# Matmuls of zeros at the head of a kernel: rounds of whole and half-array matmuls on two banks instead of twelve whole ones

## The chip, the cores and the metric

The kernel runs on one core of one Trainium2 chip. The metric is the device time of one execution in microseconds (us); the time of a kernel is the median of several executions.

A core has five engines that run side by side and wait for each other by semaphores: TensorE (PE in the profile, with its weight loads as PEld), VectorE (DVE), ScalarE (ACT), GpSimd (POOL) and SyncE (SP), which here issues the transfers.

## What is computed

One layer of a hybrid streaming encoder, for a prompt of 1024 positions and a sample of 32, with shared weights (D = 1024):

```python
hn = rmsnorm(h, g_pre)
qa, ka, va, ga, qb, kb, vb, gb = split(hn @ w_in)      # w_in: 1024 x 4096
oa = band_attention(qa, ka, va, rel_bias)              # 8 heads x 64, chunks of 64, 8 chunks back
ob = stick_breaking(qb, kb, vb)                        # 8 heads x 64, strictly causal
y  = concat(oa * silu(ga), ob * silu(gb)) @ w_out
h  = h + rmsnorm(y, g_post)
h  = h + sigmoid(h @ w_ple_gate) * (p @ w_ple)
```

The outputs are the two h and the new keys and values. All is float32. The change touches none of these values: it stands in matmuls whose results nobody reads.

## The kernel before

The function stream_step (from line 809 on it holds the whole kernel) does not issue instructions itself. Each call such as `nc.tensor.matmul` is recorded by a Recorder, which notes what each operation reads and writes; `emit` then plays them in an order that a planner finds (`order`, `simulate`): a list schedule with modelled durations, due times, and a table of offsets by engine and tile name (AHEAD_OF, AHEAD_AT). Every instruction is issued from one line, so the profile shows nearly all of them as L809, and one tells them apart by the names of their tiles.

PSUM, which matmuls write, is used as eight banks of 128 x 512. A tile of a bank is asked for with `psum(tag, name)`; the planner hands banks out as they come free, with a reserve for each tag.

The places that the prediction speaks of, in the order of PE's program:

- `zeros` (L1387, L1388): a tile of 128 x 256 that DVE sets to zero. `idle` is a bank; twelve matmuls (L1390, L1391) multiply zeros by zeros into it. They wait for DVE alone, and they are PE's first instructions.
- `ptp` (L1588 to L1591): eight transposes of the first prompt tiles of p, loaded into `pp`, against `ident`. ACT and DVE split their result into a high and a low part, `php`. The p and x tiles, weights and gains arrive by transfers that SP issues from the start on.
- `gpre` (L1818 to L1823): four matmuls that spread the gain g_pre over all partitions; they are told to follow the transposes.
- `ple` (from L1614 on): products of php with w_ple, whose two halves (`wph`, `wpl`) are made by ACT, POOL and DVE (wph0True and wpl0True among them).
- `ptx`: transposes of the normed x tiles. For each tile ACT sums squares (`be`), POOL makes the reciprocal root (`rs`), DVE scales by it and by gpre (`be<-be,rs,gpre`), and PE transposes.
- `mm_kA`, `mm_qA`, `mm_vA` and so on: the input projection, three products per weight (high by high, low by high, high by low), then between them the scores (`SA`, `SB`), the weights' transposes (`ptw`) and values (`PVA`, `PVB`) of the attention, and those of the sample (`SsA`, `PVsA`, `PVsB`). `PVsA<-newsA` and `PVsB<-newsB` multiply the 32 new positions, and so use 32 rows of the array.

The matmuls of zeros are not in the reference; they occupy PE until the first input has come.

```python
    zeros = at.tile([P, 2 * P], F32R, tag="ot", name="zeros", bufs=3)
    nc.vector.memset(f(zeros), 0.0)
    idle = psum("PV", "idle")
    for _ in range(12):
        nc.tensor.matmul(idle[:, 0:256], zeros[:, 0:P], zeros, start=True, stop=True)
```

Of the kernel before, what the change touches and what calls it, by code (L numbers as in the profile page):

```python
# [13 lines left out]
P = 128  # L14
# [3 lines left out]
T = SEQ + NS  # L18
# [4 lines left out]
HD = 64  # L23
# [791 lines left out]
def stream_step(  # L815
# [7 lines left out]
    nc = rec  # L823
# [7 lines left out]
    def psum(tag, name):  # L831
        return ps.tile([P, 512], F32, tag=tag, name=name, bufs=8)
# [554 lines left out]
    zeros = at.tile([P, 2 * P], F32R, tag="ot", name="zeros", bufs=3)  # L1387
    nc.vector.memset(f(zeros), 0.0)  # L1388
    idle = psum("PV", "idle")
    for _ in range(12):  # L1390
        nc.tensor.matmul(idle[:, 0:256], zeros[:, 0:P], zeros, start=True, stop=True)  # L1391

    def sample_attention(ab, gi):

# [774 lines left out]
    for m, (nm, src, group) in enumerate(sets):  # L2169
# [3 lines left out]
        for n, prod in enumerate(ORDER):  # L2173
            for pair, t in enumerate(group):
# [24 lines left out]
                bank = psum("S", f"{nm}{t}{prod}")  # L2199
# [126 lines left out]
```

## Time and profile before

| | |
|---|---|
| time, median of 3 runs | 753.23 us (753.18, 753.23, 753.71) |
| the profiled execution's own time | 752.74 us |
| its span, first to last instruction | 751.0 us |
| mean granted clock of TensorE | 0.998 |
| PE busy | 743.3 us, 4314 matmuls |
| DVE, ACT, POOL busy | 601.9, 532.7, 435.8 us |
| first matmul of zeros, first transpose behind them | 2.24, 4.97 us |

The profile is of one execution. A row of its timeline gives the start in us from the first instruction, the length, the engine, the tiles (written <- read), the shape, how many instructions of a kind the row merges, and, in brackets, how long the engine stood idle before it and for what. A matmul's shape such as `32*128 32x256` gives the rows and columns of the array that it uses, and then its moving operand. Matmuls overlap, so that a row's length holds the tail of its last one, and the distance between two matmuls' starts is what PE's pace is read from. A row of the stretches gives PE's, PEld's, DVE's, ACT's and POOL's busy time, the granted clock, the share of the transfer engines and GB/s.

### The profile page before, as it was taken

The page shows a single profiled execution, that of the slowest core. Times are in us where ns is not written, and L with a number is a line of the kernel's source. Part 1 is how long each engine was busy: PE and PEld are TensorE (multiplying, and loading weights), DVE is VectorE, ACT ScalarE, POOL GpSimd, SP SyncE. Part 2 cuts the span into 40 slices and gives each one's busy share as a digit, 9 for nine tenths or more (in the row PEclk, how much of TensorE's full clock was granted, in tenths as well). Part 3 has the DMA queues.
Part 4 walks back from the last instruction along what each step waited for, and adds up shares of the span by engine and source line. Part 5 has one row for each costly group of instructions (what it writes and reads, how often), then busy time and mean ns, then how long its engine had stood idle before and what let it go on. Part 6 is the DMA issues. An engine that isn't in the chain of part 4 may idle for free.

```text
span 751.0 us, 13763 instructions
## 1 busy us (share of the span) xinstructions
PE 743.3 (99%) x4314; PEld 683.5 (91%) x4314; DVE 601.9 (80%) x989; ACT 532.7 (71%) x1099; POOL 435.8 (58%) x551
## 2 busy tenths in 40 slices
PE   8999999999999999999999999999999999999997
PEld 7999999999999989999999999999997877888786
DVE  6827777889889989887989897888365878998965
ACT  5748785978877879886878866644348877784642
POOL 5723546773374742567763448687634268698623
PEclk9999999999999999999999999999999999999999
DMA  8745998868998768899788898999879847669654
GB/s 308 230 124 138 262 254 271 232 186 240 219 291 225 212 214 236 238 281 270 207 243 245 204 235 236 290 276 262 273 237 332 285 136 270 216 193 369 224 173 140
DMA packets 198971, 177.90 MB, mean 237 GB/s; under 512 B 66145, under 2 KB 158281, under 8 KB 198898
## 3 DMA queue, kind: packets, MB, share of 16 engines
q1 hardware_dynamic: 198898, 177.02, 80.8%
q8 instruction: 34, 0.56, 0.3%
q14 instruction: 39, 0.32, 0.1%
HBM read 112.01 MB, written 65.20 MB: 236 GB/s over the span
## 4 chain that ended last, share of the span: by engine, by line
PE 98%; DVE 1%; ACT 0%; issue 0%; DVEq 0%
PE mm_vA L809 6%; PE mm_kA L809 6%; PE mm_qA L809 6%; PE mm_vB L809 6%; PE mm_gB L809 6%; PE mm_kB L809 6%; PE mm_gA L809 6%; PE mm_qB L809 6%; PE SB L809 5%; PE PVB L809 4%; PE PVA L809 4%; PE SA L809 4%; PE ple L809 3%; PE o1P L809 3%; PE g1P L809 3%; PE o3P L809 3%
## 5 line engine op out<-in xcount | busy, mean ns | idle before, releaser
L809 POOL TENSOR_TENSOR be<-be 128x512 f32<-128x512 f32 (+5 forms) x98 | 92.8, 959 | 39.8 <-DVE be L809 21.6
L809 DVE TENSOR_TENSOR_SCAN be<-be,unit 128x383 f32<-128x383 f32 (+8 forms) x100 | 92.4, 945 | 12.8 <-ACT be L809 12.2
L809 ACT ACTIVATE be<-SB 128x384 f32<-128x384 f32 (+4 forms) x192 | 82.5, 501 | 15.5 <-PE SB L809 6.5
L809 DVE TENSOR_TENSOR wTl<-be,wTh 128x640 fp32r<-128x640 f32 (+4 forms) x72 | 68.4, 970 | 8.7 <-ACT wTh L809 8.4
L809 DVE STREAM_TRANSPOSE be<-be 128x640 f32<-128x640 f32 (+4 forms) x80 | 64.5, 815 | 6.0 <-POOL be L809 4.3
L809 ACT CAST wTh<-be 128x640 fp32r<-128x640 f32 (+4 forms) x72 | 50.7, 732 | 9.6 <-DMA be<-swapB 6.7
L809 ACT ACTIVATE be<-be,statA 128x640 f32<-128x640 f32 (+2 forms) x64 | 44.4, 695 | 6.2 <-DVE statA L809 6.0
L809 DVE CUSTOM_DVE_ANT_0 be<-SA,biasA 128x320 f32<-128x320 f32 (+2 forms) x64 | 29.7, 478 | 5.1 <-PE SA L809 4.6
L809 PE MATMUL SB<-kl,LB 128*128 128x384 f32 (+5 forms) x96 | 32.8, 343 | 0.0
L809 PE MATMUL SB<-kdB,LB 128*128 128x384 f32 (+5 forms) x96 | 32.7, 343 | 0.0
L809 PE MATMUL SA<-kdA,LA 128*128 128x320 f32 (+2 forms) x96 | 30.4, 318 | 0.0
L809 PE MATMUL SA<-kl,LA 128*128 128x320 f32 (+2 forms) x96 | 30.3, 319 | 0.0
L809 POOL TENSOR_TENSOR oB<-oB,oB 128x256 f32<-128x256 f32 x32 | 27.4, 875 | 4.4 <-DMA oB<-in_w_out_dram 4.3
L809 POOL TENSOR_TENSOR gB<-gB,gB 128x256 f32<-128x256 f32 x32 | 25.2, 808 | 5.9 <-DMA gB<-in_w_ple_gate_dram 5.8
L809 PE MATMUL PVB<-wTh,v2B 128*128 128x512 f32 (+2 forms) x96 | 25.9, 342 | 0.0
L809 POOL TENSOR_TENSOR kl<-stkA,kdA 64x512 fp32r<-64x512 f32 (+2 forms) x16 | 18.5, 1163 | 9.5 <-ACT kdA L809 7.2
L809 POOL TENSOR_TENSOR h<-h,x 128x512 f32<-128x512 f32 (+1 forms) x18 | 23.0, 1299 | 1.4 <-DVE h L809 1.2
L809 PE MATMUL PVB<-wTl,v2B 128*64 128x128 f32 (+2 forms) x96 | 23.0, 348 | 0.0
L809 PE MATMUL mm_kB<-hnl,wh_kB 128*128 128x352 f32 x96 | 22.4, 333 | 0.0
L809 POOL TENSOR_TENSOR kl<-stkB,kdB 64x512 fp32r<-64x512 f32 x16 | 18.3, 1159 | 7.1 <-ACT kdB L809 4.0
L809 PE MATMUL mm_qA<-hnl,wh_qA 128*128 128x352 f32 x96 | 22.1, 332 | 0.0
L809 PE MATMUL PVA<-wTl,v2A 128*64 128x128 f32 (+1 forms) x96 | 22.1, 312 | 0.0
(678 smaller groups left out, 2562.6 us busy)
## 6 DMA issues: line engine op xcount, KB each, us to landing
swapB<-be SPq DMA_DIRECT2D x16, 448.0 KB, 4.5
be<-swapB SPq DMA_DIRECT2D x64, 112.0 KB, 3.4
swapA<-be SPq DMA_DIRECT2D x8, 640.0 KB, 3.6
swapA<-be SPq DMA_DIRECT2D x16, 320.0 KB, 5.1
be<-swapA SPq DMA_DIRECT2D x32, 160.0 KB, 5.4
be<-swapA SPq DMA_DIRECT2D x64, 80.0 KB, 3.8
oB<-in_w_out_dram SPq DMA_DIRECT2D x16, 256.0 KB, 5.2
sum_dro<-oB SPq DMA_DIRECT2D x16, 256.0 KB, 3.2
```

The costliest lines, as they stand in the source:

```text
L809: getattr(getattr(tc.nc, o.what[0]), o.what[1])(*args, **kw)
```

## The change

The twelve matmuls become three rounds of four on two banks: a whole one into `idle`, a whole one into `other`, then one on rows 0 to 63 into `idle` and one on rows 64 to 127 into `other`. HD is 64. Columns, weights' width and the moving 256 columns stay as they are.

```diff
     idle = psum("PV", "idle")
-    for _ in range(12):
-        nc.tensor.matmul(idle[:, 0:256], zeros[:, 0:P], zeros, start=True, stop=True)
+    other = psum("T", "other")
+    for _ in range(3):
+        for bank, r in ((idle, slice(0, P)), (other, slice(0, P)), (idle, slice(0, HD)), (other, slice(HD, P))):
+            nc.tensor.matmul(bank[:, 0:256], zeros[r, 0:P], zeros[r], start=True, stop=True)
```

On all engines the other instructions keep their order and, but for one, their waits. The first place is PE's start. Before, with the waits in brackets (DMAHW: a transfer; ptp_254 and ptp_265 are the two banks of transposes):

```order
L809 MATMUL idle<-zeros 128x256 [waits DVE_49]
L809 MATMUL idle<-zeros 128x256 x11
L809 MATMUL ptp_254<-ident,pp_180 128x128 [waits DMAHW0_49,Pool_49]
L809 MATMUL ptp_254<-ident,pp_180 128x128 x3
L809 MATMUL ptp_265<-ident,pp_180 128x128 [waits DMAHW2_49]
```

Now, from the last of the three rounds on; these rows give the written side's shape, so the third and fourth, which are the halves, read like the whole ones:

```order
L809 MATMUL idle<-zeros 128x256
L809 MATMUL other<-zeros 128x256
L809 MATMUL idle<-zeros 128x256
L809 MATMUL other<-zeros 128x256
L809 MATMUL ptp_264<-ident,pp_180 128x128 [waits DMAHW0_49,Pool_49]
L809 MATMUL ptp_264<-ident,pp_180 128x128 x3
L809 MATMUL ptp_266<-ident,pp_180 128x128 [waits DMAHW2_49]
```

Nothing behind the zeros has moved; the number of matmuls is the same.

The second place is PE's first products of ple, a few instructions on (ple_0_307 and ple_0_308 before are ple_0_308 and ple_0_309 now). Before:

```order
L809 MATMUL ple_0_307<-wph0True,php_190 128x512 [waits Activation_49]
L809 MATMUL ple_0_307<-wph0True,php_190 128x512 [waits DVE_49]
L809 MATMUL ple_0_308<-wph0True,php_190 128x512 x2
L809 MATMUL ple_0_315<-wph0True,php_192 128x512 [waits Activation_49]
L809 MATMUL ple_0_315<-wph0True,php_192 128x512 [waits DVE_49]
```

Now:

```order
L809 MATMUL ple_0_308<-wph0True,php_190 128x512 [waits Activation_49]
L809 MATMUL ple_0_308<-wph0True,php_190 128x512 [waits DVE_49]
L809 MATMUL ple_0_309<-wph0True,php_190 128x512 [waits PE_49]
L809 MATMUL ple_0_309<-wph0True,php_190 128x512
L809 MATMUL ple_0_316<-wph0True,php_192 128x512 [waits Activation_49]
```

The banks are handed out differently, now that two are taken at the start, and ple_0_309 gets the one of `idle`; it waits for the last matmul of zeros into it.

## The prediction

> **What bounds the kernel now.** I read the first page first: the share of each engine and the chain that ended last.
>
> ```profile
> span 751.0 us, 13763 instructions
> PE 743.3 (99%) x4314; PEld 683.5 (91%) x4314; DVE 601.9 (80%) x989; ACT 532.7 (71%) x1099; POOL 435.8 (58%) x551
> PE 98%; DVE 1%; ACT 0%; issue 0%; DVEq 0%
> ```
>
> TensorE (PE) is busy for 743.3 of 751.0 us and carries 98% of the chain, so whatever makes PE late by some time at the start makes the end late by that time, unless PE later waits for something that did not move. The waits of PE behind the first 20 us, and the two places they stand at, are:
>
> ```profile
> PE SsA L809 <- DVE QhlsA L809: 0.5, 1, 0.5
> PE mm_vA L809 <- ACT stvA L809: 0.2, 1, 0.2
> ...
> 411.71 0.39 PE L809 MATMUL SsA<-Kh0sA,QhlsA 128*128 128x272 f32 x1 [0.46 <-DVE QhlsA L809]
> ...
> 266.73 0.59 PE L809 MATMUL mm_vA<-hnh,wh_vA 128*128 128x352 f32 x2 [0.19 <-ACT stvA L809]
> ```
>
> Together 0.65 us (0.46 + 0.19): the most that could be absorbed later. Next I read the timeline of PE in the first 30 us, since the change stands at its first row.
>
> ```profile
> 2.24 2.93 PE L809 MATMUL idle<-zeros 128*128 128x256 f32 x12 [2.24 <-DVE zeros L809]
> 4.97 1.91 PE L809 MATMUL ptp<-ident,pp 128*128 128x128 f32 x8
> 6.53 1.64 PE L809 MATMUL gpre<-wTl,ones 128*128 128x512 f32 x4
> 8.00 1.55 PE L809 MATMUL ple<-wph0True,php 128*128 128x512 f32 x6
> 9.39 0.86 PE L809 MATMUL ple<-wpl0True,php 128*128 128x512 f32 x3
> ...
> 14.50 0.60 PE L809 MATMUL ptx<-ident,be 128*128 128x128 f32 x4
> ...
> 19.48 1.08 PE L809 MATMUL ptx<-ident,be 128*128 128x128 f32 x8
> 20.32 0.71 PE L809 MATMUL ple<-wph0True,php 128*128 128x512 f32 x2
> ```
>
> PE runs without a hole from 2.24 us. Its rate changes, though. Eight transposes took 4.97 to 6.53, 0.195 us each; eight of the same form took 19.48 to 20.32, 0.105 each. Twelve matmuls of zeros, 256 columns, took 2.73 us; six matmuls of 512 columns took 8.00 to 9.39, 0.232 each, which is 0.116 for 256. So PE works at half its rate at first. The four gpre matmuls took 1.47 us, between 4 x 0.427 (half rate) and 4 x 0.232: c/0.427 + (1.47 - c)/0.232 = 4 gives c = 1.19 us at half rate, so the rate doubles at about 7.7 us, some 5.5 us after the first matmul. The granted clock of the page does not show this (it reads 1.00 there); it shows the way back at the end:
>
> ```profile
> 743.00:746.00 3.00, 3.00 (x26) 2.91 (x24) 1.71 (x3) 0.81 (x2) 1.55 (x2) 1.00 0.24 89
> 746.00:748.23 2.23, 0.17 (x2) 0.00 (x0) 1.86 (x5) 0.57 (x2) 0.79 (x1) 1.00 0.26 96
> 748.24:748.26 0.02, 0.00 (x0) 0.00 (x0) 0.02 (x1) 0.00 (x0) 0.00 (x0) 0.50 1.84 717
> ```
>
> PE stops at 746.17 (0.17 us into the second stretch), and at 748.24 the clock falls to 0.50: the half rate is a clock gate that follows PE's activity.
>
> **The change part by part.** The instructions of all engines keep their order; only the twelve matmuls change, and one wait is added (the first ple_0_309 waits for the last zeros on its bank). That producer is done some 2 us earlier, so I cost the wait at nothing. So the change is a matter of two numbers: when the zeros end, and when the gate opens.
>
> (a) *Whole against half, switching.* Six times now PE goes from all 128 rows to fewer or back (three rounds, in and out, the last way out to ptp). The trace has no matmul on 64 rows, but some on 32, between whole ones:
>
> ```profile
> 213.64 0.28 PE L809 MATMUL PVsA<-Vl2sA,whsA 128*128 128x256 f32 x1
> 213.76 0.28 PE L809 MATMUL PVsA<-Vh2sA,wlsA 128*128 128x256 f32 x1
> ...
> 271.35 0.28 PE L809 MATMUL PVsB<-Vh2sB,wlsB 128*128 128x256 f32 x1
> 271.56 0.38 PE L809 MATMUL PVsB<-newsB 32*128 32x256 f32 x1
> 271.86 0.43 PE L809 MATMUL mm_vA<-hnh,wl_vA 128*128 128x352 f32 x1
> 272.22 0.50 PE L809 MATMUL PVsB<-newsB 32*128 32x256 f32 x2
> 272.65 0.60 PE L809 MATMUL mm_vA<-hnl,wh_vA 128*128 128x352 f32 x2
> ...
> 271.55 0.18 PEld L809 LDWEIGHTS PVsB<-newsB 32*128 32x128 f32 x1 [0.17 <-issue]
> ```
>
> Whole to whole, 256 columns take 0.12 us (213.64 to 213.76). Across a change of rows, start to start is 0.21 (271.35 to 271.56): 0.09 more. The weights are then loaded only at 271.55, not ahead of time, and the matmul behind them lasts 0.38 instead of 0.28: 0.10 more. So a switch costs about 0.19 us at the full clock. At half clock the exposed load is shown by the first zeros matmul, which had nothing ahead of it:
>
> ```profile
> L809 PEld LDWEIGHTS idle<-zeros x12: 288/330/333, 2.2 to 4.5; 128*128 128x128 f32 x12
> L809 PE MATMUL idle<-zeros x12: 415/415/582, 2.2 to 4.8; 128*128 128x256 f32 x12
> ```
>
> 582 against 415 ns is 0.167 us; the others are (2.73 - 0.167) / 12 = 0.213 apart. The stop itself lies between 0.09 (full clock) and 0.415 - 0.213 = 0.20 (the whole tail of a matmul); I take 0.11, near the first, the only one measured at a switch. So 6 x (0.11 + 0.167) = 1.66 us; bounds 6 x 0.19 = 1.14 and 6 x 0.367 = 2.20.
>
> (b) *Two halves side by side.* The second half's rows are others than the first's, so it may run beside it: a pair saves between nothing and 0.213 us. If its load follows the first half's by 0.167, it starts 0.167 instead of 0.213 later and saves 0.046; I take that, 3 x 0.046 = 0.14, bounds 0 and 0.64. [...]
>
> (c) *Sum.* The zeros end 1.66 - 0.14 = 1.5 us later, ptp starts at 6.47 (bounds: 1.14 - 0.64 = 0.5 and 2.2 later). Up to the gate's opening at 7.7 all of that is work at half rate, and PE does it afterwards in half the time: PE is 0.75 us late (0.25 to 1.1), if the gate opens when it did. The other way, a shorter row of zeros would be of use, since its successor is not waiting for data:
>
> ```profile
> 0.72 0.40 SPq L809 DMA_DIRECT2D pp<-in_p_prompt_dram  x1
> ...
> 1.53 0.35 SPq L809 DMA_DIRECT2D pp<-in_p_prompt_dram  x1
> DMA to landing us min/median/max: 2.6/2.9/3.2
> ```
>
> The two loads of pp have landed by 0.72 + 3.2 = 3.9 and 1.53 + 3.2 = 4.7 at the latest, before 4.97.
>
> What hangs behind ptp is late by more than PE: ACT's first cast of php, with it the casts and subtractions on POOL, by 1.5 us.
>
> ```profile
> 7.25 1.29 POOL L809 TENSOR_TENSOR wpl0True<-wpr_0True,wph0True 128x512 fp32r<-128x512 f32 x1 [5.44 <-ACT wph0True L809]
> 11.58 0.72 POOL L809 TENSOR_SCALAR rs<-ms 128x1 f32<-128x1 f32 x1
> 12.99 1.41 DVE L809 SCALAR_TENSOR_TENSOR be<-be,rs,gpre 128x512 f32<-128x512 f32 x2
> 14.11 0.22 POOL L809 TENSOR_SCALAR rs<-ms 128x1 f32<-128x1 f32 x1 [1.16 <-ACT be L809]
> ```
>
> POOL works through from 7.25 to rs at 11.58, so the first half of DVE's scaling (12.99 to 13.7) would end at about 15.2; PE wants it for ptx at 14.50 + 0.75 = 15.25. The cover just holds; for each 0.1 us that the zeros are later still, 0.05 is added there. POOL's idle 1.16 us before 14.11 takes up the rest.
>
> PE's own time: 752.74 us (span 751.0 and 1.7 around it) + 0.75 = 753.5. The median of the runs shown is 753.23, 0.49 above that execution, so I put **754.0** against it.
>
> **The rivals.**
>
> *The gate opens later (slower).* With six stops, PE streams about 2.4 us of the 4.2 us of zeros. Place: the clock from 2.24 to 12 us. It decides if the gate wants unbroken work: steady work opened it after 5.5 us, and an idle 2.07 us (746.17 to 748.24) closed it. If those 5.5 count from the last switch at 6.47, it opens at 12.0 instead of 7.7; PE does 4.3 us at half rate, 2.1 us of work lost, with 0.75 about 2.9: 756.1. For it: the work before the opening was entirely unbroken. Against: ptp and gpre, most of what came before the opening, are unchanged. [...]
>
> *Halves run side by side and switching is free.* The zeros are 0.64 us shorter, PE 0.3 ahead: 752.9. The rows at 271 us speak against it.
>
> *The lateness is absorbed* at 266.73 and 411.71: at most 0.65, 753.3. Against it: what PE waits for there comes from PE's own earlier work.
>
> *The gate opens earlier*, as the halves might count as more activity: PE is then held by x; ptx cannot start before DVE's 13.7, 0.8 earlier than 14.50: 752.4. Nothing in the trace speaks for it.
>
> **How the numbers follow.** Forecast 0.48 (753.23 + 0.25 to + 1.1: 753.5 to 754.3); gate later 0.34; free switching 0.11; absorbed 0.05; gate earlier 0.02. What a measurement of this kernel can tell from no change is about 0.2%, 1.5 us. Slower by more: the late gate and a little of the forecast's upper end, 0.38. Faster by more: 0.02, what is left for an earlier gate whose gain x does not hold back. Within: 0.60, the rest. The range leaves out the two cases below 753.1 (0.13) and reaches to the late gate: 753.1 to 756.1.
>
> **What would show it.** Right: idle matmuls on 64 rows in the timeline, the stretch from the first zeros to ptp 4.2 us instead of 2.73, ple's first row near 8.75, and every later stage late by the same 0.75. If ple's six take 2.6 us (0.43 each) instead of 1.39, the gate is late. If ptp starts before 4.97, switching is free and the forecast wrong in sign. If a later stage differs by another amount than ple's first row, the lateness was absorbed or grew.

## The result, and the profile after

| | before | after |
|---|---|---|
| median of 6 runs each, us | 753.20 (752.38 to 754.25) | 755.52 (754.69 to 757.21) |
| ratio after / before | | 1.0032, 95% interval 1.0019 to 1.0045 |
| profiled execution, its span | 752.74, 751.0 | 755.65, 753.9 |

The change makes the kernel slower by 2.4 us (0.0032 x 753.2; 1.4 to 3.4 by the interval). The time lies inside the range that was given, 1.5 us above the forecast. First the page of after: span, busy time, and the head of the chain of work that ended last.

```profile
span 753.9 us, 13763 instructions
PE 745.4 (99%) x4314; PEld 683.8 (91%) x4314; DVE 600.8 (80%) x989; ACT 532.4 (71%) x1099; POOL 435.9 (58%) x551
PE 94%; DVE 2%; DMA 2%; ACT 1%; issue 1%; DVEq 0%; ACTq 0%; SPq 0%
```

The other engines' busy time is as before within about 1 us. PE is busy for 2.1 us more (745.4 against 743.3), and the chain leaves PE for some more of its way (94% instead of 98%): two things to look for. PE's timeline at the start of after, and a later row of before to compare with:

```profile
2.24 0.58 PE L809 MATMUL idle<-zeros 128*128 128x256 f32 x1 [2.24 <-DVE zeros L809]
2.62 0.41 PE L809 MATMUL other<-zeros 128*128 128x256 f32 x1
2.97 0.58 PE L809 MATMUL idle<-zeros 64*128 64x256 f32 x1
2.97 0.58 PE L809 MATMUL other<-zeros 64*128 64x256 f32 x1
3.48 0.58 PE L809 MATMUL idle<-zeros 128*128 128x256 f32 x1
...
4.71 0.58 PE L809 MATMUL idle<-zeros 128*128 128x256 f32 x1
...
5.94 1.97 PE L809 MATMUL ptp<-ident,pp 128*128 128x128 f32 x8
7.56 2.05 PE L809 MATMUL gpre<-wTl,ones 128*128 128x512 f32 x4
9.41 2.16 PE L809 MATMUL ple<-wph0True,php 128*128 128x512 f32 x6
11.42 0.86 PE L809 MATMUL ple<-wpl0True,php 128*128 128x512 f32 x3
...
23.11 1.46 PE L809 MATMUL mm_kA<-hnh,wh_kA 128*128 128x352 f32 x8
```

```profile
21.10 1.46 PE L809 MATMUL mm_kA<-hnh,wh_kA 128*128 128x352 f32 x8
```

A round takes 1.23 us (3.48 to 4.71), where four whole matmuls took 4 x 0.213 = 0.85. The two halves of a pair start together (both at 2.97). ptp starts at 5.94 instead of 4.97. Before, the six matmuls of ple ran at full rate from the first on (8.00 to 9.39, 1.39 us); now they take 9.41 to 11.42, 2.01 us, and gpre's four take 1.85 (7.56 to 9.41) instead of 1.47. So PE works at half rate (0.43 us from one matmul of 512 columns to the next, 8.99 to 9.41, against 0.232 at full rate before) for longer: it is 0.97 us late at ptp, 1.41 at ple's first row, 2.03 at ple's next rows (11.42 against 9.39), and still 2.01 at mm_kA (23.11 against 21.10). From there to 409 us it stays at 2.0 to 2.1.

The gate's closing can be seen in the stretches of time at the end (us, then busy time of PE, PEld, DVE, ACT, POOL, granted clock, DMA share, GB/s):

```profile
748.50:751.42 2.92, 0.57 (x5) 0.36 (x4) 2.10 (x6) 0.78 (x2) 1.18 (x1) 1.00 0.31 112
751.42:751.44 0.02, 0.00 (x0) 0.00 (x0) 0.00 (x0) 0.00 (x0) 0.00 (x0) 0.60 1.06 358
```

It closes at 751.42, before at 748.24. The trace also has a record of the moments at which the granted clock changes, from which the opening can be read: 7.55 us before, 10.73 after. PE's pace bears the record out: the opening of after falls among ple's six, which take 2.01 us, neither the 1.39 of full rate nor the 2.6 of half rate. Opening and closing moved by the same 3.18 us; the experiments say why.

The second place where the traces part lies in the middle. PE's waits in after, the row of the longer one, and the same row of before:

```profile
PE SA L809 <- DVE wlsA L809: 1.2, 1, 1.2
PE mm_vA L809 <- ACT stvA L809: 0.2, 1, 0.2
...
427.40 0.39 PE L809 MATMUL SA<-kdA,LA 128*128 128x320 f32 x1 [1.16 <-DVE wlsA L809]
```

```profile
424.70 0.31 PE L809 MATMUL SA<-kdA,LA 128*128 128x320 f32 x1
```

The wait of 0.46 for QhlsA at 411.71 is gone, so that there PE is only 1.37 late; in its place it waits 1.16 for wlsA before 427.40 (424.70 before, 2.70 earlier), and is 2.9 late from 434 us to the end. So of the 2.9 us of this pair of executions, 2.03 arise in the first 12 us, 0.80 between 409 and 434 us, and the rest between 266 and 280 us.

### The profile page after: what moved, and what is told of

Its sections match the earlier page's. It is cut to its first block, busy times and chain, and to the rows that moved or that the text cites. A ratio compares the mean times of both kernels' runs of the same rounds, so it can differ in the third digit from the quotient of the medians.

```text
span 753.9 us, 13763 instructions
## 1 busy us (share of the span) xinstructions
PE 745.4 (99%) x4314; PEld 683.8 (91%) x4314; DVE 600.8 (80%) x989; ACT 532.4 (71%) x1099; POOL 435.9 (58%) x551
## 4 chain that ended last, share of the span: by engine, by line
PE 94%; DVE 2%; DMA 2%; ACT 1%; issue 1%; DVEq 0%; ACTq 0%; SPq 0%
PE mm_vA L809 6%; PE mm_kA L809 6%; PE mm_qA L809 6%; PE mm_vB L809 6%; PE mm_gB L809 6%; PE mm_gA L809 6%; PE mm_kB L809 5%; PE mm_qB L809 5%; PE SB L809 5%; PE PVB L809 4%; PE PVA L809 4%; PE ple L809 3%; PE SA L809 3%; PE o1P L809 3%; PE g1P L809 3%; PE o3P L809 3%
## 5 line engine op out<-in xcount | busy, mean ns | idle before, releaser
L809 ACT CAST wTh<-be 128x640 fp32r<-128x640 f32 (+4 forms) x72 | 50.7, 733 | 11.1 <-DMA be<-swapB 6.9
```

The source lines that it names most:

```text
L809: getattr(getattr(tc.nc, o.what[0]), o.what[1])(*args, **kw)
```

## The experiments

Ten runs were made, two of them with the kernels after and before unchanged. The theory in question, an assumption of the author's that the runs are to test: **the gate looks at PE's activity in windows of fixed length that run on their own; it opens at the end of the first window with enough of it, and rounds with stops don't have enough.** Its rivals: the gate opens after a fixed time or amount of work, wherever that begins; matmuls of zeros, or on half the rows, don't count as activity; the second bank or the longer zeros cost the time by themselves. (A step below is such a window.)

The record of the clock in each run's own trace gives for every kernel when it went up and came down. The last two columns are worked out: the share of a step of 3.413 us in which PE streamed columns, that is without stops and without loads that nothing covers, for the step at whose end the clock went up and for the step ahead of that one.

| kernel | up, us | down, us | down - up, in steps of 3.413 us | share, step that ended with the opening | share, step ahead |
|---|---|---|---|---|---|
| before | 7.55 | 748.24 | 217.0 | 0.99 | 0.50 |
| before, once more (e8) | 8.25 | 748.94 | 217.0 | 0.99 | 0.71 |
| after | 10.73 | 751.42 | 217.0 | 0.99 | 0.69 |
| after, once more (e7) | 9.53 | 750.22 | 217.0 | 0.99 | 0.51 |
| e1, two banks | 6.68 | 750.78 | 218.0 | 1.00 | 0.25 |
| e2, grouped | 6.81 | 750.91 | 218.0 | 0.76 | 0.29 |
| e3, seventeen | 6.81 | 750.91 | 218.0 | 1.00 | 0.29 |
| e4, zeros first | 5.29 | 749.40 | 218.0 | 0.96 | 0.16 |
| e5, rounds early | 7.26 | 751.36 | 218.0 | 0.85 | 0.39 |
| e6, all halves | 6.36 | 750.46 | 218.0 | 0.95 | 0.16 |
| e9, seven rounds | 16.44 | 757.13 | 217.0 | 0.99 | 0.66 |
| e10, forty | 6.68 | 754.20 | 219.0 | 1.00 | 0.57 |

The length of a step comes from the table itself: the distances from up to down take only three values, 740.692 us (five times), 744.106 (six times) and 747.519 (once). They lie 3.41 apart, and 740.692 is 217 times 3.4133. So in twelve executions the distance is a whole number of such steps, though PE's work begins and ends at different times from kernel to kernel. In these executions the clock thus changed at the ends of such steps, and the kernel's work did not set their place: in after and e7, the same kernel, it went up at 10.73 and 9.53. None of the steps above with a share up to 0.71 opened it, every one from 0.76 on did.

**e1_two_banks.** Twelve whole matmuls, on two banks in turn.

```diff
-    for _ in range(12):
-        nc.tensor.matmul(idle[:, 0:256], zeros[:, 0:P], zeros, start=True, stop=True)
+    other = psum("T", "other")
+    for _ in range(6):
+        for bank in (idle, other):
+            nc.tensor.matmul(bank[:, 0:256], zeros[:, 0:P], zeros, start=True, stop=True)
```

> Twelve whole matmuls of zeros as before, but alternating between the two banks: the new bank alone, without halves. Theory 1 (the switch between whole and half costs time, and the stops keep the clock gate shut for longer): nothing changes, ptp starts at 4.97 us, ple's first row at 8.0, time within 0.5 us of before. Rival (the second bank and the wait that it brings to ple cost the time): ptp or ple later, time some 2 us above before.

Measured: 753.46 us against 753.46 of before, ratio 0.9998 (0.9989 to 1.0006); ptp at 4.97 as before. ple's first row stands at 7.61 instead of the expected 8.0, since the clock went up at 6.68. The second bank, the banks' other distribution and the added wait cost nothing.

**e2_grouped.** The same twelve, but the six whole ones first, then the three pairs: two switches instead of six.

```diff
-    for _ in range(12):
-        nc.tensor.matmul(idle[:, 0:256], zeros[:, 0:P], zeros, start=True, stop=True)
+    other = psum("T", "other")
+    for r in ((slice(0, P), slice(0, P)), (slice(0, HD), slice(HD, P))):
+        for _ in range(3):
+            for bank, x in zip((idle, other), r):
+                nc.tensor.matmul(bank[:, 0:256], zeros[x, 0:P], zeros[x], start=True, stop=True)
```

> The same twelve matmuls as in the change, six whole and three pairs of halves, but the six whole ones first: two switches instead of six. By the distances in the profile of the change (0.345 us into a pair, 0.51 from a pair to a whole one) ptp starts near 4.75 us. Theory 1 (stops keep the gate shut): the gate opens as before, ple's first row near 7.9, time 0 to 0.3 us below before. Rival (halves count as less activity for the gate, however they are laid): the gate opens one step of 3.2 to 3.4 us later, PE about 1.6 us late, time some 1.5 to 2.5 us above before.

Measured: 753.65 against 753.46, ratio 0.9999 (0.9990 to 1.0008). Pairs next to each other, in PE's timeline of e2:

```profile
3.82 0.58 PE L809 MATMUL idle<-zeros 64*128 64x256 f32 x1
3.83 0.58 PE L809 MATMUL other<-zeros 64*128 64x256 f32 x1
4.20 0.41 PE L809 MATMUL idle<-zeros 64*128 64x256 f32 x1
4.20 0.41 PE L809 MATMUL other<-zeros 64*128 64x256 f32 x1
4.42 0.41 PE L809 MATMUL idle<-zeros 64*128 64x256 f32 x1
4.42 0.41 PE L809 MATMUL other<-zeros 64*128 64x256 f32 x1
4.76 2.23 PE L809 MATMUL ptp<-ident,pp 128*128 128x128 f32 x8
```

Pairs without a switch between them follow each other by 0.22, the pace of whole ones, and only the first of them pays the load (0.58 instead of 0.41). So the switches are what a round costs, not the halves. ptp starts 0.21 earlier than before, and there it waits for its data: the whole row of ptp takes 1.94 us until gpre starts (6.70) instead of 1.56, and in the trace the weight load of the fifth transpose stands idle for 0.46 us until the second load of pp has landed, 4.4 us after its issue. In this profile nothing is gained: PE loses 0.78 between 12 and 17 us in short stops, the last of them a wait for the scaled x.

**e3_seventeen.** Whole matmuls as before, seventeen instead of twelve: the zeros end when those of the change do, without a switch.

```diff
-    for _ in range(12):
+    for _ in range(17):
```

> Seventeen whole matmuls of zeros instead of twelve: ptp is as late as in the change (2.24 + 0.17 + 17 x 0.213 = 6.03 us), but PE works without a stop. Theory 1 (stops keep the gate shut): the gate opens as before, PE is 1.06 us of half-rate work late, 0.5 us behind ple, time 0.5 us above before. Rival (zeros do not count for the gate, what opens it is the real work from ptp on): the gate opens near 10.7 us as in the change, PE 2 us late, time 2 to 3 us above before.

```profile
2.24 4.00 PE L809 MATMUL idle<-zeros 128*128 128x256 f32 x17 [2.24 <-DVE zeros L809]
6.04 1.42 PE L809 MATMUL ptp<-ident,pp 128*128 128x128 f32 x8
7.21 1.17 PE L809 MATMUL gpre<-wTl,ones 128*128 128x512 f32 x4
8.22 1.71 PE L809 MATMUL ple<-wph0True,php 128*128 128x512 f32 x6
```

Measured: 753.73 against 753.46, ratio 1.0000 (0.9991 to 1.0009). In PE's timeline of e3 ptp starts later than in after (6.04), and yet gpre's four run at full rate (1.01 us) where after's take 1.85. The clock is up at 6.81, and PE's pace changes there: up to 6.67 the transposes start 0.21 apart, from 6.85 on 0.11. So zeros do count, and their mere length is not what costs 2.4 us: as long a stretch without switches can't be told from before (the interval is -0.7 to 0.7 us). Whether the expected 0.5 us is there, these runs don't show.

**e4_zeros_first** sets the memset of zeros first on DVE, by the table of offsets; the zeros are those of before. **e5_rounds_early** is the change with the same edit.

```diff
-    ('DVE', 'news'): -180, ('DVE', 'ot'): 1301, ('DVE', 'v'): 3181, ('DVE', 'zeros'): 1745,
+    ('DVE', 'news'): -180, ('DVE', 'ot'): 1301, ('DVE', 'v'): 3181, ('DVE', 'zeros'): -9000,
```

> The kernel before with the memset of zeros ahead of DVE's other memset (0.91 us): the twelve matmuls start at 1.33 instead of 2.24 us and end at 4.06. Theory 1 with a gate that counts the work from its start: it opens 0.9 us earlier, at about 6.6, and PE is 0.9 us ahead at ptp; time 0.5 to 0.9 us below before. With a gate that judges fixed stretches: the opening stays at 7.5 or jumps to 4.1, time 0.4 or 1 to 1.5 us below before. Rival (zeros do not count): the opening follows ptp, time 0.5 to 0.9 us below before.

> The change's three rounds, but with the memset of zeros ahead of DVE's other memset, so that the first matmul starts at 1.17 us and ptp at 1.17 + 3.70 = 4.87, as early as in the kernel before (4.97): the late ptp is taken away and the stops stay. Theory 1 (a gate that opens after a stretch of about 3.4 us in which PE was busy for most of the time, with stops that spoil such a stretch): it opens between 6.5 and 9.9, on the mean 1.7 us later than in the kernel before; time 0.5 to 1.3 us above before. Rival (the stops do not touch the gate, only the late ptp costs): time within 0.3 us of before.

Measured: e4 753.43 against 753.46, ratio 0.9999 (0.9990 to 1.0008); e5 753.88 against 753.42, ratio 1.0006 (0.9997 to 1.0016). PE's timeline of e4, and then of e5:

```profile
1.17 2.93 PE L809 MATMUL idle<-zeros 128*128 128x256 f32 x12 [1.17 <-DVE zeros L809]
3.90 1.78 PE L809 MATMUL ptp<-ident,pp 128*128 128x128 f32 x8
...
13.57 0.63 PE L809 MATMUL ptx<-ident,be 128*128 128x128 f32 x4 [0.17 <-DVE be L809]
```

```profile
4.88 1.97 PE L809 MATMUL ptp<-ident,pp 128*128 128x128 f32 x8
6.49 1.51 PE L809 MATMUL gpre<-wTl,ones 128*128 128x512 f32 x4
7.85 1.55 PE L809 MATMUL ple<-wph0True,php 128*128 128x512 f32 x6
```

e4 starts 1.07 us sooner and its gate opens at 5.29; at 12 us PE is 1.25 ahead of before. Then it waits for x (13.57) and is 0.90 ahead, of which 0.56 goes between 409 and 434 us, so that 0.34 is left at the end of this profile. The runs show no gain where 0.5 to 0.9 us was expected; the interval, -0.8 to 0.6 us, leaves room for most of it. In e5 ptp stands 0.09 ahead of before, with the change's rounds: the gate opened at 7.26, within a step that held two of the switches (share 0.85). So it does not want unbroken work. The time of e5 lies between before and after, and its interval (-0.2 to 1.2 us) takes in both the 0.5 to 1.3 us of the theory and the rival's 0.3: it does not decide between them, and only says that at least half of the 2.4 us is gone where the same rounds stand 1.07 us sooner. What speaks against that rival, a late ptp as the only cost, is e3, where ptp is as late, and e9 below.

**e6_all_halves.** Twelve pairs of halves instead of twelve whole matmuls: 24 matmuls, one switch.

```diff
+    other = psum("T", "other")
     for _ in range(12):
-        nc.tensor.matmul(idle[:, 0:256], zeros[:, 0:P], zeros, start=True, stop=True)
+        for bank, r in ((idle, slice(0, HD)), (other, slice(HD, P))):
+            nc.tensor.matmul(bank[:, 0:256], zeros[r, 0:P], zeros[r], start=True, stop=True)
```

> Twelve pairs of halves instead of twelve whole matmuls: the same length, one switch (to ptp) instead of six. ptp starts 0.3 us later than before (one way out, 0.13 + 0.05, and the first pair), near 5.2 us. Theory 1 (stops, not halves, keep the gate shut): the gate opens between 4.8 and 8.2 as before, time within 0.5 us of before. Rival (half-array matmuls count as half the activity): the gate opens only after a stretch of ptp and whole matmuls, at 7.9 to 11.3, time 1.5 to 2 us above before.

Measured: 753.21 against 753.42, ratio 0.9997 (0.9986 to 1.0008). In PE's timeline of e6:

```profile
4.76 0.41 PE L809 MATMUL idle<-zeros 64*128 64x256 f32 x1
4.76 0.41 PE L809 MATMUL other<-zeros 64*128 64x256 f32 x1
5.11 1.68 PE L809 MATMUL ptp<-ident,pp 128*128 128x128 f32 x8
```

Halves side by side cost what one whole matmul does (0.214 from pair to pair, 2.62 to 4.76 for ten), and the one switch puts ptp 0.14 later (5.11). The gate opened at 6.36: pairs of halves count.

**e7_change_again and e8_before_again.** The kernels after and before once more, unchanged, for a second reading of the gate.

> The change once more, for a second reading of the gate. Theory 1, with stretches of 3.41 us that begin at any time and need a busy share between 0.71 and 0.86: it opens somewhere from 7.6 to 11.0 us. Rival (PE's 5.3 us of work in the kernel before, counted from the last stop): it opens at 11.2 each time, and in the first reading, 10.73, nearly so.

> The kernel before once more, for a second reading of the gate. Theory 1: it opens somewhere from 4.8 to 8.2 us, as in the kernels with unbroken zeros (6.68 to 6.81 so far). Rival (a fixed time of work): at 7.5 as in the first reading. The time moves by half of the difference.

PE's rows of e7, then of e8:

```profile
7.57 2.05 PE L809 MATMUL gpre<-wTl,ones 128*128 128x512 f32 x4
9.42 1.61 PE L809 MATMUL ple<-wph0True,php 128*128 128x512 f32 x6
...
22.57 1.46 PE L809 MATMUL mm_kA<-hnh,wh_kA 128*128 128x352 f32 x8
```

```profile
6.54 1.95 PE L809 MATMUL gpre<-wTl,ones 128*128 128x512 f32 x4
8.33 1.55 PE L809 MATMUL ple<-wph0True,php 128*128 128x512 f32 x6
...
21.41 1.46 PE L809 MATMUL mm_kA<-hnh,wh_kA 128*128 128x352 f32 x8
```

Times of one execution each: 754.12 and 752.66. The work is the same as in the first readings to 0.01 us up to gpre, and yet the clock went up 1.20 us sooner in e7 (9.53) and 0.70 later in e8 (8.25). So no fixed time or amount of work opens it. PE's lateness at mm_kA follows: 22.57 against 21.10 is 1.47, 21.41 against 21.10 is 0.31. The end of e8 does not follow it (752.66 against 752.74, where half of the difference was expected), since e8 gains 0.44 between 409 and 434 us.

**e9_seven_rounds** has seven rounds instead of three, **e10_forty** forty whole matmuls instead of twelve (the planner now sets the memset earlier, and the last three behind the first transposes). The first diff is e9's against after, the second e10's against before.

```diff
-    for _ in range(3):
+    for _ in range(7):
         for bank, r in ((idle, slice(0, P)), (other, slice(0, P)), (idle, slice(0, HD)), (other, slice(HD, P))):
```

```diff
-    for _ in range(12):
+    for _ in range(40):
```

> The change with seven rounds instead of three: PE works with stops, about half of the time streaming, for 8.7 us (7 x 1.23 + 0.16), until ptp at 11.0 us. Theory 1 (a stretch of 3.41 us opens the gate only if PE streams for more than some 0.76 to 0.86 of it): all zeros run at half clock, every round takes 1.23 us, and the gate opens between 12.6 and 16.1. Rival (the gate opens some 4 to 5.5 us after PE's first work, stops or not, and the two late openings of the change were accidents): it opens between 6 and 8.2, and the later rounds take little more than half as long.

> Forty whole matmuls without a stop, which begin at 1.17 us, since the planner now puts their memset first. Theory 1: the gate opens in their midst, 2.6 to 6.0 us after they begin, so at 3.8 to 7.2; their distance goes from 0.213 to 0.12 us there. A rival in which zeros do not count: all forty at 0.213 us, ptp at 9.9.

PE's timeline of e9, then of e10:

```profile
10.88 1.11 PE L809 MATMUL ptp<-ident,pp 128*128 128x128 f32 x4
11.93 0.58 PE L809 MATMUL other<-zeros 64*128 64x256 f32 x1
12.44 1.11 PE L809 MATMUL ptp<-ident,pp 128*128 128x128 f32 x4
13.20 2.06 PE L809 MATMUL gpre<-wTl,ones 128*128 128x512 f32 x4
15.05 2.20 PE L809 MATMUL ple<-wph0True,php 128*128 128x512 f32 x6
17.09 0.86 PE L809 MATMUL ple<-wpl0True,php 128*128 128x512 f32 x3
```

```profile
1.17 7.11 PE L809 MATMUL idle<-zeros 128*128 128x256 f32 x37 [1.17 <-DVE zeros L809]
8.12 0.60 PE L809 MATMUL ptp<-ident,pp 128*128 128x128 f32 x4
```

Measured, one execution each: 761.03 and 755.83 against 753.39. In e9 the rounds went on for 8.6 us (2.24 to 10.88), two and a half steps, and the gate stayed shut; it opened at 16.44, four us after the last switch (12.44), a little beyond what was expected, since the planner set one half behind the first transposes and so two switches more. In a round PE streams 3 x 0.213 of 1.23 us, 0.52; such work did not open the gate in all of that time. In e10 whole matmuls of zeros alone opened it, at 6.68.

## Why the prediction was right, and where it was wrong

**The mechanism** was named: PE bounds the kernel, PE starts at half rate, and what the change does is to move the end of the zeros and the opening of the gate. The range held because it reached to the late gate; the forecast itself, 753.5 to 754.3, was missed. **The step that failed** is in the sum (c): "PE is 0.75 us late (0.25 to 1.1), if the gate opens when it did", which was given 0.48 and made the forecast. The gate did not open when it did. What spoke for that, "ptp and gpre, most of what came before the opening, are unchanged", overlooked what the twelve executions show, that the opening was decided over one step of 3.41 us: in after the step from 3.91 to 7.32 held 2.0 us of rounds ahead of ptp and came to 0.69, so the next one had to be waited for.

**Its terms.**
- (a) A switch was put at 0.11 + 0.167. Measured in after: the pair starts at 2.97 and the next whole matmul at 3.48, 0.51 later, of which 0.213 is the stream; 0.30 is left. In six switches that is near enough; the last, into ptp, cost less: the load that shows there is 0.05, by the distance from the first transpose to the second (0.265 instead of 0.213).
- (b) was mis-sized. The halves start together instead of 0.167 apart, so each pair saves the whole 0.213: 0.64, the bound, instead of 0.14. The row of the 32-row matmuls could not show it. The starts are 3 to 4 ns apart in after, and at most 0.01 us in the pairs of the other kernels.
- (c) So the zeros end 0.97 later instead of 1.5, inside 0.5 to 2.2, and half of it counts: 0.49 instead of 0.75.
- Smaller readings: the gate of before opened at 7.55, not at about 7.7; and a transpose takes 0.213 at half rate, not 0.195, since gpre's first row starts only 0.07 behind the last transpose. That pp has landed by 4.7 at the latest held for that execution alone; in e2 the second load took until 5.9.

**The rival that came** is the late gate, given 0.34 at 756.1. It rested on unbroken work, 5.5 us counted from the last switch, which would have opened at 12.0. The opening was at 10.73 and 9.53, and e5 shows that work need not be unbroken. What decided in these runs was the share of a step: up to 0.71 did not open the gate, from 0.76 on did. The idle 2.07 us that the prediction took to close the gate is no fixed time either: the clock fell 2.07 (before) to 4.94 us (e10) after PE's last matmul.

**The sum as the runs show it.** Work at half rate is counted at half (in e3 the transposes stand 0.21 apart ahead of the opening and 0.11 behind it), so PE's lateness behind the gate is half of what ptp is late plus half of what the gate is late. For after: 0.97/2 + 3.18/2 = 2.08, measured 2.03. For e7: 0.98/2 + 1.98/2 = 1.48, measured 1.47. For e8: 0.70/2 = 0.35, measured 0.31. For e1: -0.87/2 = -0.43, measured -0.39. For e5: -0.09/2 - 0.29/2 = -0.19, measured -0.17. The sum leaves waits out. In e2, e3, e4 and e6 weight loads of PE stand idle for data in the first 12 us (0.46 for pp in e2; 0.27 and 0.22 for wph0True and php in e3; 0.27 and 0.42 for pp and wTl in e4; 0.17 for php in e6), and at 12 us PE is 0.1 to 0.4 later than by the sum.

For the mean over executions an estimate: if the steps lie evenly and the bound is 0.74, between the 0.71 and 0.76 above, before's stream (from 2.41 us) has 0.74 of a step, 2.52 us, first at 4.9 us, so the gate opens between 4.9 and 8.3; its readings (before, e1, e3, e6, e8) were 6.36 to 8.25. After's has it first at about 7.7, with 0.52 up to ptp and 1 from there, so the gate opens between 7.7 and 11.1; read at 10.73 and 9.53. The middles are 2.8 us apart: 0.49 + 1.4 = 1.9 us, within the measured 1.4 to 3.4. By the same estimate one kernel's executions differ by up to half of 3.4 us, 1.7. The six times of before spread over 1.9, those of after over 2.5, and 33 of before in another set of runs over 2.75 (752.25 to 755.00), so the steps are not all of the scatter; the stretch from 409 to 434 us is a part of it.

**Absorption** at 411.71, given 0.05, is not shown. PE's lateness fell from 2.10 to 1.37 there, but not because PE came late: e4 and e6, which come there 0.90 and 0.29 us ahead of before, have no wait there either and move by the same 0.7. The wait belongs to some executions and not to others (before 0.46, e1 0.41, e8 0.24, none in the rest), and after's 0.73 was given back at 427.40. This place is no part of the change: from 409 to 434 us the kernels with whole zeros moved by +0.82 (e1), +0.35 (e3), +0.56 (e4) and -0.44 (e8) against the profile of before, after by +0.80 and e7, the same kernel, by -0.12. **Free switching** and an **earlier gate** fell with the first row of ptp and of ple. POOL's cover of the scaled x held: no wait stands at ptx in after.

**Open:** what lets PE wait in the one or the other place between 409 and 434 us; where between 0.71 and 0.76 the bound lies, and whether loads count a little (the shares rest on one way of counting); whether a half without its partner counts in full; and, with one or two profiles of each kernel, whether the steps do lie evenly, which the estimate of the mean rests on. No version that was run is faster than before by more than can be measured.

## What to carry to other kernels

In these runs TensorE's clock opened at the end of a step of 3.41 us in which PE, filler work included, streamed for 0.76 or more, and did not with 0.71 or less. At half rate a round that changed between all rows and half of them stopped for 0.13 and showed its load for 0.17 at each change and streamed half the time (3 x 0.213 of 1.23 us), and seven such rounds (e9) did not open the gate. Put equal shapes next to each other; twelve pairs of halves cost what twelve whole matmuls did (e6, 753.21 against 753.42 us). And in two readings of each kernel the clock went up at 7.55 and 8.25 us (before) and at 10.73 and 9.53 (after), and by the estimate above one kernel's executions differ by up to 1.7 us (half of 3.4) without any change: read the gate's opening in more than one profile before you put a difference down to an edit.

## What the runs showed of the hardware

- The clock's changes lie 217, 218 or 219 x 3.413 us apart within an execution, in twelve of twelve; their place against the kernel's start differed from execution to execution (up at 7.55 and 8.25 us in two of before, at 10.73 and 9.53 in two of after).
- The gate opened with PE streaming for 0.76 of a step (e2) and stayed shut with 0.71 (e8).
- The gate closed at the end of a step in which PE was busy for 0.39 (before, 744.83 to 748.24) and stayed open over a step with 0.55 (e10, 747.38 to 750.79), a share below the 0.71 that did not open it (e8).
- Work with hardly a stop from the first matmul on opened it after 4.1 us (e4: 1.17 to 5.29) at the earliest and 6.0 us (e8: 2.25 to 8.25) at the latest.
- Matmuls on rows 0 to 63 and on rows 64 to 127 started 3 to 4 ns apart in after and at most 0.01 us in e2, e5, e6, e7 and e9, and a pair took 0.214 us at half rate (e6), where one whole matmul took 0.213 (before).
